# A 128-byte tile moved from the first working pool to the last one: a Fourier and Hyena encoder layer on one core

## The chip, the core and the metric

The kernel runs on one core of a Trainium2 chip. The metric is the device time of one execution in microseconds (us). Three runs of the kernel before took 2387.26, 2387.34 and 2389.71 us; their median is 2387.34 us.

## What is computed

The reference is one encoder layer, applied to two inputs of 1024 rows and 1024 channels, all in float32. Cut to what matters:

```python
p = rmsnorm(x, g_pre) @ w_in                       # 1024 x 8192: fv, fg, hv (3 parts), hg, mg (2 parts)
fz = fftn(fv in 4 groups of 256, over rows and group).real
y_f = (fz * silu(fg)) @ w_fourier_out
v, x1, x2 = split(short_conv(hv, w_short), 3)      # width 3 along the rows
z = x1 * long_conv(v, filter 0);  z = x2 * long_conv(z, filter 1)
y_h = (z * silu(hg)) @ w_hyena_out
g_f, g_h = split(sigmoid(mg + b_merge), 2)
out = x + rmsnorm((g_f * y_f + g_h * y_h) @ w_out, g_post)
```

The two long convolutions have filters as long as the sequence in both directions; the kernel makes them with small Fourier transforms written as matrix products.

## The kernel before

Every large product is made in three matmuls: a number is split into a high and a low part, and high times high, high times low and low times high are summed in PSUM (`mm3`, and `times` in the tail; both end in `mm`, line 193, so line 193 is the line of nearly all matmuls in the profile). ScalarE rounds the high part (line 170), and VectorE or GpSimd subtracts to get the low part (line 180).

There are three stages. `phase_fourier` makes the Fourier branch's transform. `phase_main` makes the filters and, in `branches`, the Hyena branch of both inputs. It also makes most input projections: `inproj` takes a stationary operand of 128 x 128 out of the tiles `wh` and `wl` (high and low part of a piece of `w_in`) and a moving operand of 128 x 512 out of the tiles `x`, which hold the whole normalised input, high and low, for all of the stage. One call has 48 such matmuls; they write the PSUM tile `pin`. `phase_tail` makes the rest with a scheme of seven block products instead of eight: the PSUM tile is `pg` for the last projections of the second input and for the output product, and `pn` for the two branches' output products. In the tail the stationary operands lie either in the old tiles `wh`, `wl` and `w`, or in others (`s1h`, `s1l`, ... `s4l`, `a2h`, `a2l`, `wa`; for `pn` in halves of the old `x` tiles and in two tiles `st0`, `st1`; the profile calls these `wh` and `wl` too, since the tile's own name is that). The moving operands are the tiles called `x`, `oB`, `n` and `room`.

What matters for the change is where these tiles lie in a partition of SBUF. The kernel opens memory pools, and the program puts each pool behind the one opened before it; inside a pool the tiles follow each other in the order in which they are first asked for. The order and the sizes per partition are:

- `cp`, constants, to byte 17,760;
- `wp`, opened by `open_x`: `wh` (3 buffers of 2048 bytes), `wl` (3 of 2048), `w` (2 of 2048), `gt` (3 of 2048), `mark` (1 of 128);
- `xp`, opened by `open_x` too: sixteen tiles of 4096 bytes, `x00` to `x17`, each with a high half and a low half of 2048 bytes;
- in `phase_main`: `mf`, `wa`, `wb`, `mi`. `mi` is the last, with `cinv` (18,432 bytes) and `cin0` (2048);
- in `phase_tail`, at the same place behind `xp`: `gs` (four `room` tiles of 16,384 bytes), `gw`, `gr`, `gt`, `op`.

A stationary operand takes 512 bytes of a partition and starts at a multiple of 512 bytes from its pool's first tile; a moving one of 512 columns takes 2048 bytes. `wp` without `mark` has 22,528 bytes, eleven times 2048. With the 128 bytes of `mark`, `xp` and all pools behind it start at 128 bytes past a multiple of 2048 from `wp`. So the distance from the stationary operand to the moving one, taken modulo 512, is:

- operands out of `wh`, `wl`, `w` of `wp` (`pin`, and two of the seven block products of `pg`): 384, that is 128 bytes short of a multiple of 512;
- all other matmuls of 512 columns (`pn`, and the other five block products of `pg`): 0, since both operands lie behind `mark`.

`mark` itself is a trick of order. The list `self.due` holds copies between tensors in DRAM that GpSimd has to issue one at a time. In `branches`, after each of the first 30 steps, GpSimd copies one column of the step's result into `mark` (line 1101) and only then issues the next copy of the list. Nobody reads `mark`.

Of the kernel before, what the change touches and what calls it, by code (L numbers as in the profile page):

```python
# [10 lines left out]
F32R = mybir.dt.float32r  # L11
# [5 lines left out]
P = 128  # L17
# [143 lines left out]
class K:  # L161
# [824 lines left out]
    def phase_main(self, nct=8, nb=NB, nf=16):  # L986
        tc, nc, a = self.tc, self.nc, self.a
        with ExitStack() as es:
            pool = lambda n: es.enter_context(tc.tile_pool(name=n, bufs=1, reuse_waits="tile"))
            self.open_mm(es, "psm")  # L990
            mf, wa, wb, mi = pool("mf"), pool("wa"), pool("wb"), pool("mi")
            ws = Rooms(wa, wb)
            with tc.issue_after(self.fz_stored.ins):
                self.load_x(0, range(4))
            self.hid = ws.tile([P, L], F32R, tag="q", name="hid", bufs=2)
            hid = ws.tile([P, L], F32, tag="q", name="hidr", bufs=2)
            for i in range(2):
                nc.sync.dma_start(hid[64 * i:64 * i + 64].rearrange("p (n t) -> p n t", n=2),
                                  self.d_h.rearrange("(n p) t -> p n t", n=2))
            with tc.issue_after(self.third[0].ins), tc.issue_after(self.third[1].ins):  # L1000
                nc.scalar.copy(self.hid, hid)
                self.sub("dve", self.hid[64:128], hid[64:128], self.hid[64:128])
            taps = self.filter_taps(0, 0, self.filter_rates(0, 0, ws), ws)
            self.load_x(0, range(4, 8))
            self.cfw0 = mf.tile([P, 4 * P], F32, name="cfw0")
            self.cfwd = mf.tile([P, 2, 12 * P], F32R, name="cfwd")
            nc.sync.dma_start(self.cfw0, a["c_fw0"])
            nc.gpsimd.tensor_copy(self.cfwd[:, 0, 0:1], self.X[4][0][1][:, 0:1])
            nc.gpsimd.dma_start(self.cfwd, a["c_fwd"])
            plain = [(5, c) for c in range(8)] + [(6, c) for c in range(8)] + [(4, c) for c in range(NH)]  # L1010
            fill = sorted([((2 * c + 1) / len(plain), t) for c, t in enumerate(plain)]
                          + [((2 * c + 1) / max(NF, 1), (0, c)) for c in range(NF)])
            fill = [t for _, t in fill]
            rates = self.filter_rates(1, 0, ws)
            self.due = self.weight_sums()
            room = mi.tile([P, 2, INVW], F32, tag="cinv", name="sums", bufs=1).rearrange("p a b -> p (a b)")
            for i in range(nf):
                if i in (3, 5, 7, 9):
                    k = (i - 3) // 2
                    r = room[:, 2048 * (k % 2):2048 * (k % 2) + 2048].rearrange("p (q n) -> p q n", q=4)  # L1020
                    self.block_sums([r[:, q] for q in range(4)], 0, k, [self.d_x[1][k + 4 * j] for j in range(2)])
                nxt = self.filter_taps((i + 1) % 2, (i + 1) // 2, rates, ws) if i + 1 < nf else None
                self.filter_spectrum(i % 2, i // 2, taps, ws)
                if i + 2 < nf:
                    rates = self.filter_rates(i % 2, i // 2 + 1, ws, self.rounded)
                taps = nxt
                for sec, c in fill[i * len(fill) // nf:(i + 1) * len(fill) // nf]:
                    self.spill_gate(0, sec, c, ws)
                if i == 12:
                    self.cinv = mi.tile([P, 2, INVW], F32R, tag="cinv", name="cinv", bufs=1)  # L1030
                    self.cin0 = mi.tile([P, 4 * P], F32, name="cin0")
                    nc.sync.dma_start(self.cin0, a["c_in0"])
                if 12 <= i < 15:

                    s = slice((i - 12) * INVW // 3, (i - 11) * INVW // 3)
                    nc.gpsimd.dma_start(self.cinv[:, :, s], a["c_inv"][:, :, s])
            self.branches(nb, nct, ws)

    def branches(self, nb, nct, ws):

        tc, nc = self.tc, self.nc
        steps = []
        for b in range(nb):
            steps.append((b, 0, 0))
            for c in range(1, nct):
                steps += [(b, 0, c), (b, 1, c - 1)]
            steps.append((b, 1, nct - 1))
        plain = list(self.PLAIN)  # L1050
        Z, X, G = {}, {}, {}

        def front(i):
            b, n, c = steps[i]
            src = self.conv(1, c, ws, "v", b) if n == 0 else Z.pop(c)
            return self.conv_front(src, ws)

        def gates(i):
            b, n, c = steps[i]
            x = self.conv(2 + n, c, ws, f"x{n + 1}", b)  # L1060
            if n and b == 0:
                early = c < NH
                ps = None if early else self.inproj(4, c)
                sg = [self.wp.tile([P, 512], F32, tag="gt", name="sg", bufs=3) for q in range(2)]
                for q in range(2):
                    s = slice(512 * q, 512 * q + 512)
                    if early:
                        nc.sync.dma_start(sg[q], self.d_g[0][4][c][:, s])
                    else:
                        nc.scalar.activation(sg[q], ps[:, s], AF.Silu)  # L1070
                G[i] = sg, early
            X[i] = x

        def close(i):

            if i in G:
                sg, early = G.pop(i)
                for q in range(2):
                    s = slice(512 * q, 512 * q + 512)
                    if early:  # L1080
                        with tc.issue_after(self.rounded.ins):
                            nc.scalar.activation(sg[q], sg[q], AF.Silu)
                    self.mul("dve", X[i][:, s], X[i][:, s], sg[q])
        B = front(0)
        gates(0)
        for i, (b, n, c) in enumerate(steps):
            nxt = None
            if i + 1 < len(steps):
                nxt = front(i + 1)
                gates(i + 1)  # L1090
                if i + 2 < len(steps) and steps[i + 2][0] != steps[i + 1][0]:
                    self.load_x(steps[i + 2][0])
            y = self.conv_back(n, c, B, ws)
            close(i + 1)
            B = nxt
            for _ in range({4: 1, 3: 1, 2: 2, 1: 2}.get(len(steps) - i, 0)):
                self.spill_gate(b, *plain.pop(), ws)
            z = self.gate(n, c, y, X.pop(i))
            if self.due:
                mark = self.wp.tile([P, 32], F32R, tag="mark", name="mark", bufs=1)  # L1100
                with tc.issue_after(nc.gpsimd.tensor_copy(mark[:, 0:1], z[:, 0:1]).ins):  # L1101
                    self.due.pop(0)()
            if n == 0:
                Z[c] = z
                continue
            nc.sync.dma_start(self.d_sh[b][c], z)
            if b == 0 and NF <= c:
                self.spill_gate(0, 0, c, ws)
        with tc.issue_after(self.ended.ins):
            for sec, c in plain:  # L1110
                self.spill_gate(1, sec, c, ws)
# [605 lines left out]
```

## Time and profile before

| | before |
|---|---|
| median of three runs | 2387.34 us |
| the profiled execution's own time | 2390.22 us |
| its span, first to last instruction | 2388.4 us |
| mean granted TensorE clock | 0.997 |
| TensorE matmul busy | 2339.0 us (98%) |
| VectorE busy | 1967.7 us (82%) |
| ScalarE busy | 1118.6 us (47%) |
| GpSimd busy | 446.4 us (19%) |
| matmuls of 128 x 512 into `pin` | 4224 |
| into `pn` | 1344 |
| into `pg` | 1680 |

A row of a group reads: line, engine, operation, tile written <- tiles read (for a matmul first the moving, then the stationary operand), shape, count; then the busy time of the group in us (overlaps counted once), the mean length of one in ns, and the idle time of the engine ahead of them. Matmuls overlap: one of 512 columns is shown some 390 ns long, and the next starts some 230 ns after it. The pitch from start to start is therefore read from the chain of waits, where a stretch of matmuls of one kind has its length and its count.

### The profile page before, as it was taken

How to read it: one execution, taken by the hardware profiler on the slowest of the kernel's cores; microseconds unless marked ns; L12 is line 12 of the kernel's file. 1: busy time of each engine (PE TensorE's matmuls, PEld its weight loads, DVE VectorE, ACT ScalarE, POOL GpSimd, SP SyncE). 2: the span in 40 equal slices, each digit the busy share in tenths (PEclk: the TensorE clock that was granted, in tenths of full speed). 3: DMA queues.
4: the chain of work that ended last, by engine and by line, in shares of the span. 5: the costliest groups of instructions: out<-in, count | busy, mean ns of one | idle time of the engine just before them, and what ended most of it. 6: DMA issues, size and time to landing. Idle time of an engine off the chain costs nothing.

```text
span 2388.4 us, 36206 instructions
## 1 busy us (share of the span) xinstructions
PE 2339.0 (98%) x12784; PEld 2019.5 (85%) x12784; DVE 1967.7 (82%) x3438; ACT 1118.6 (47%) x2080; POOL 446.4 (19%) x428
## 2 busy tenths in 40 slices
PE   6999999999999999999999999999999999999998
PEld 5989788888878888888888888888888888888787
DVE  7775687888788999999898999997765578787987
ACT  6645576676753333334222222333443464656443
POOL 3342222122223333332000000122000000101311
PEclk9999999999999999999999999999999999999999
DMA  7636765554566567667465565444954678998654
GB/s 254 208 139 218 260 212 174 177 172 151 175 218 204 186 211 211 209 194 246 161 194 150 171 193 158 151 159 159 347 165 137 221 257 267 273 313 246 198 159 141
DMA packets 246207, 479.69 MB, mean 201 GB/s; under 512 B 24582, under 2 KB 82280, under 8 KB 245706
## 3 DMA queue, kind: packets, MB, share of 16 engines
q1 hardware_dynamic: 222013, 402.25, 51.7%
q0 software_dynamic: 23792, 75.11, 11.1%
q8 instruction: 100, 1.64, 0.3%
q14 instruction: 81, 0.66, 0.1%
q10 hardware_dynamic: 221, 0.04, 0.0%
HBM read 326.82 MB, written 177.73 MB: 211 GB/s over the span
## 4 chain that ended last, share of the span: by engine, by line
PE 55%; DVE 4%; DMA 1%; issue 1%; ACT 0%; POOL 0%; DVEq 0%; SPq 0%; POOLq 0%; ACTq 0%
PE pin L193 19%; PE pg L193 14%; PE pn L193 12%; PE pT L193 5%; PE pX L193 5%; PE tph L904 1%; DMA xr<-in_x 1%; DVE x L176 0%; DMA d_m<-gt 0%; DMA k<-d_k 0%; DVE t L180 0%; DVE b L180 0%; DVE y L180 0%; DVE wl L180 0%; DVE o L176 0%
## 5 line engine op out<-in xcount | busy, mean ns | idle before, releaser
L193 PE MATMUL pin<-x,wh 128*128 128x512 f32 x2816 | 900.3, 395 | 0.0
L193 PEld LDWEIGHTS pin<-x,wh 128*128 128x128 f32 x2816 | 525.2, 189 | 107.8
L193 PE MATMUL pin<-x,wl 128*128 128x512 f32 x1408 | 556.8, 396 | 0.0
L180 POOL TENSOR_TENSOR wl<-wr,wh 128x512 fp32r<-128x512 f32 x128 | 223.5, 1747 | 696.1 <-ACT wh L170 661.3
L193 PEld LDWEIGHTS pin<-x,wl 128*128 128x128 f32 x1408 | 265.4, 189 | 52.7
L193 PE MATMUL pn<-room,wh 128*128 128x512 f32 x864 | 266.2, 389 | 0.0
L193 PEld LDWEIGHTS pn<-room,wh 128*128 128x128 f32 x864 | 162.1, 188 | 33.9 <-DVE gt L180 0.2
L193 PE MATMUL pn<-room,wl 128*128 128x512 f32 x432 | 168.4, 390 | 0.1
L180 DVE TENSOR_TENSOR t<-pX,k 128x1024 f32<-128x1024 f32 x128 | 155.6, 1215 | 11.0 <-PE pX L193 7.1
L193 PE MATMUL pX<-bh,cfwd 128*128 128x256 f32 x768 | 162.3, 288 | 0.0
L193 PE MATMUL pT<-cinv,yh 128*128 128x256 f32 x768 | 145.4, 284 | 1.9 <-DVE T0s L180 1.9
L170 ACT CAST wh<-wr 128x512 fp32r<-128x512 f32 x128 | 79.2, 618 | 135.8 <-PE pin L193 106.6
L170 ACT CAST bh<-b 128x512 fp32r<-128x512 f32 x144 | 88.3, 620 | 114.1 <-DVE b L180 83.7
L193 PEld LDWEIGHTS pT<-cinv,yh 128*128 128x128 f32 x768 | 122.7, 190 | 9.1 <-ACT T1s L957 2.0
L193 PEld LDWEIGHTS pX<-bh,cfwd 128*128 128x128 f32 x768 | 127.0, 190 | 2.7 <-issue 0.2
L1358 POOL DMA_DIRECT2D d_m<-gt x32 | 27.1, 848 | 531.9 <-DVE gt L180 502.7
L170 ACT CAST yh<-y 128x512 fp32r<-128x512 f32 x96 | 59.6, 621 | 132.2 <-DVE y L180 132.2
L193 PE MATMUL pX<-bl,cfwd 128*128 128x256 f32 x384 | 109.0, 284 | 0.0
L193 PE MATMUL pT<-cinv,yl 128*128 128x256 f32 x384 | 108.9, 284 | 0.0
L180 DVE TENSOR_TENSOR bl<-b,bh 128x512 fp32r<-128x512 f32 x144 | 103.7, 724 | 4.0 <-ACT bh L170 3.8
L1101 POOL CAST mark<-x 128x1 fp32r<-128x1 f32 x30 | 21.1, 704 | 415.6 <-DVE x L176 415.5
L180 DVE TENSOR_TENSOR y<-t 128x512 f32<-128x512 f32 x128 | 90.9, 710 | 6.8 <-PE pT L193 6.4
(362 smaller groups left out, 5174.6 us busy)
## 6 DMA issues: line engine op xcount, KB each, us to landing
k<-d_k SPq DMA_DIRECT2D x128, 512.0 KB, 4.3
wr<-in_w_in SPq DMA_DIRECT2D x128, 256.0 KB, 3.5
d_g<-gt SPq DMA_DIRECT2D x124, 256.0 KB, 2.9
wl<-d_s SPq DMA_DIRECT2D x56, 512.0 KB, 5.7
d_k<-kt SPq DMA_DIRECT2D x128, 128.0 KB, 2.2
d_k<-kt SPq DMA_DIRECT2D x64, 256.0 KB, 2.7
g<-d_g SPq DMA_DIRECT2D x64, 256.0 KB, 5.5
r<-d_g SPq DMA_DIRECT2D x60, 256.0 KB, 5.9
```

Of the source, the lines that this page charges most:

```text
L170: self.rounded = nc.scalar.copy(h, src)
L180: return e.tensor_tensor(out, a, b, op=op)
L193: return self.nc.tensor.matmul(out, lhsT, rhs, start=start, stop=stop, skip_group_check=shared)
L904: nc.tensor.transpose(tp[:, q * P:(q + 1) * P], eo[:, e, q], self.ident)
L1101: with tc.issue_after(nc.gpsimd.tensor_copy(mark[:, 0:1], z[:, 0:1]).ins):
L1358: nc.gpsimd.dma_start(dst, t, accum_op=ADD)
```

## The change

The tile `mark` goes from `wp` to `mi` and from 32 columns to the one that is used. `mi` is handed to `branches` for that.

```diff
-            self.branches(nb, nct, ws)
-
-    def branches(self, nb, nct, ws):
+            self.branches(nb, nct, ws, mi)
+
+    def branches(self, nb, nct, ws, mi):
...
             if self.due:
-                mark = self.wp.tile([P, 32], F32R, tag="mark", name="mark", bufs=1)
-                with tc.issue_after(nc.gpsimd.tensor_copy(mark[:, 0:1], z[:, 0:1]).ins):
+                mark = mi.tile([P, 1], F32R, tag="mark", name="mark", bufs=1)
+                with tc.issue_after(nc.gpsimd.tensor_copy(mark, z[:, 0:1]).ins):
                     self.due.pop(0)()
```

The program has the same instructions in the same order on each engine, with the same waits: the copy was of one column before too. What differs is addresses. `wp` stays where it was (the first `wh` buffer at byte 17,760), and everything behind it lies 128 bytes lower: the first `x` tile at byte 40,288 instead of 40,416, `room0` and `cfw0` at 105,824 instead of 105,952. `mark` now lies behind `cin0`, at byte 229,216, where nothing comes after it in `phase_main`. All matmuls of 512 columns of the last two stages have their two operands at a multiple of 512 bytes from each other then, and the starts of the tiles `wh`, `wl` and `x` are multiples of 2048 bytes apart. Distances among the tiles behind `wp` are as before.

## The prediction

> **What bounds the kernel now.** I start with the busy times of the page, then with the chain that ended last, to see which engine sets the end.
>
> ```profile
> PE 2339.0 (98%) x12784; PEld 2019.5 (85%) x12784; DVE 1967.7 (82%) x3438; ACT 1118.6 (47%) x2080; POOL 446.4 (19%) x428
> PE 55%; DVE 4%; DMA 1%; issue 1%; ACT 0%; POOL 0%; DVEq 0%; SPq 0%; POOLq 0%; ACTq 0%
> ```
>
> TensorE is busy for 98% of the span, and of the time that the chain puts on an engine nearly all is TensorE's. A busy share can hide waits, so the second view is what TensorE waited for between 200 us and the end; it has six lines in all, and these are the longest:
>
> ```profile
> PE pXf L193 <- DVE b L180: 5.5, 1, 5.5
> PE pn L765 <- DVE acc L180: 2.2, 1, 2.2
> PE pg L193 <- ACT u L1242: 1.9, 2, 1.4
> PE pT L193 <- DVE T0s L180: 1.9, 1, 1.9
> ```
>
> That is 12 us in 2200. So whatever makes matmuls shorter in that stretch shortens the kernel, unless another engine is just behind. The third view is the groups of TensorE by shape, and in it the change's subject can be seen before anything is changed:
>
> ```profile
> L193 PE MATMUL pin<-x,wh 128*128 128x512 f32 x2816 | 900.3, 395 | 0.0
> L193 PE MATMUL pin<-x,wl 128*128 128x512 f32 x1408 | 556.8, 396 | 0.0
> L193 PE MATMUL pn<-room,wh 128*128 128x512 f32 x864 | 266.2, 389 | 0.0
> L193 PE MATMUL pn<-room,wl 128*128 128x512 f32 x432 | 168.4, 390 | 0.1
> ```
>
> All four are matmuls of one shape at one granted clock. Those into `pin` take their weights from `wp` and last 395 and 396 ns; those into `pn` take them from behind `mark` and last 389 and 390 ns. The stages differ too, so this alone proves nothing. In `pg` both kinds stand in one stage, in turn:
>
> ```profile
> L193 PE MATMUL pg<-x,wh 128*128 128x512 f32 x176 | 55.3, 395 | 0.0
> L193 PE MATMUL pg<-oB,wh 128*128 128x512 f32 x120 | 37.7, 395 | 0.0
> L193 PE MATMUL pg<-x,wl 128*128 128x512 f32 x88 | 34.8, 395 | 0.0
> L193 PE MATMUL pg<-oB,wl 128*128 128x512 f32 x60 | 23.8, 397 | 0.6 <-DVE wl L180 0.6
> L193 PE MATMUL pg<-oB,w 128*128 128x512 f32 x12 | 3.0, 394 | 0.0
> L193 PE MATMUL pg<-x,s4h 128*128 128x512 f32 x96 | 29.6, 390 | 0.0
> L193 PE MATMUL pg<-oB,s4h 128*128 128x512 f32 x64 | 19.7, 390 | 0.0
> L193 PE MATMUL pg<-room,s2h 128*128 128x512 f32 x160 | 49.3, 389 | 0.0
> L193 PE MATMUL pg<-x,wa 128*128 128x512 f32 x24 | 5.6, 391 | 0.0
> ```
>
> The data `x` and `oB` occur with both kinds of weights. With `wh`, `wl` and `w` (distance 384 modulo 512) they last 394 to 397 ns, with `s4h` and `wa` (distance 0) 390 to 391 ns. So the place of the weights goes with the length, and the data, the stage and the kind of work do not. The view of the tile `pg` gives least, median and most of one matmul and of its weight load:
>
> ```profile
> L193 PEld LDWEIGHTS pg<-x,wh x176: 187/188/192, 1700.5 to 1897.7; 128*128 128x128 f32 x176
> L193 PE MATMUL pg<-x,wh x176: 390/394/404, 1700.8 to 1898.0; 128*128 128x512 f32 x176
> L193 PEld LDWEIGHTS pg<-room,s3h x160: 187/188/188, 1695.1 to 2371.0; 128*128 128x128 f32 x160
> L193 PE MATMUL pg<-room,s3h x160: 389/389/389, 1695.3 to 2371.2; 128*128 128x512 f32 x160
> ```
>
> Two things are to be seen. The weight loads have the same median, 188 ns, so loading from `wp` is not slower by itself. And the matmuls at distance 0 are all 389 ns, while those at distance 384 run from 390 to 404. An unsteady length in the matmul, with a steady load, looks like two reads that meet: the stream of moving data and the load of the next weights, which run at the same time. What decides then is how the two addresses stand to each other, and that is what the change sets.
>
> **What a matmul of 512 columns costs in time.** The lengths overlap, so the pitch decides. Three stretches of the chain, with start, length, and count:
>
> ```profile
> 1659.61 27.66 PE pin L193 x119
> 1687.28 224.92 PE pg L193 x984
> 1934.47 271.69 PE pn L193 x1198
> ```
>
> For `pin` 27.66 / 119 is 232.4 ns; for `pn` 271.69 / 1198 is 226.8 ns; `pg`, which has both kinds, lies between with 228.6 ns. The difference of the pure ones is 5.6 ns, about the 6 ns by which the lengths differ.
>
> **The sum.** First term: 4224 matmuls into `pin` (2816 + 1408) at 5.6 ns are 23.7 us. Second term: in `pg` the rows with `wh`, `wl` and `w` count 176 + 120 + 88 + 60 + 12 = 456, at 5.6 ns 2.6 us. Together 26.3 us; with 6 ns in place of 5.6 they are 28.1 us, which is the upper end.
>
> Third term, a loss: in `phase_main` the scheduler puts matmuls into `pin` in short stretches between narrower ones, and no row shows how a 512-column matmul at distance 0 fares beside those. The nearest row is `pg<-oB,s4h`, 390 ns on the average where the undisturbed ones have 389: it follows the products out of `wp`, and the difference is what a change of stream leaves behind. Bounds are nothing, and 1 ns on each of the 4224 matmuls, which is 4.2 us; I take 1.7 us, nearer to nothing, since much of that 1 ns comes from the old distance and goes with it.
>
> Fourth term: VectorE. Where TensorE becomes shorter, VectorE has to keep up. The windows of 100 us show where that is tight (window, then TensorE, its loads, VectorE, ScalarE, GpSimd):
>
> ```profile
> 700.00:800.00 100.00, 100.00 (x579) 87.56 (x578) 86.08 (x139) 37.10 (x69) 29.78 (x35) 1.00 0.62 198
> 800.00:900.00 100.00, 100.00 (x591) 88.09 (x590) 99.91 (x153) 36.03 (x67) 41.59 (x44) 1.00 0.64 201
> 900.00:1000.00 100.00, 98.13 (x591) 86.36 (x590) 96.87 (x152) 33.66 (x61) 27.91 (x36) 1.00 0.71 215
> 1000.00:1100.00 100.00, 100.00 (x586) 87.75 (x586) 100.00 (x162) 36.37 (x68) 35.48 (x36) 1.00 0.65 191
> 1100.00:1200.00 100.00, 100.00 (x569) 87.05 (x568) 90.47 (x150) 34.40 (x62) 5.80 (x7) 1.00 0.61 208
> 1500.00:1600.00 100.00, 100.00 (x599) 88.39 (x598) 97.95 (x167) 33.66 (x64) 19.79 (x15) 1.00 0.52 164
> ```
>
> And the same windows with the matmuls into `pin` alone, for their counts:
>
> ```profile
> 800.00:900.00 100.00, 65.94 (x271) 49.42 (x270) 15.22 (x12) 6.54 (x6) 1.00 0.64 201
> 900.00:1000.00 100.00, 62.22 (x249) 44.92 (x248) 12.73 (x11) 5.57 (x5) 1.00 0.71 215
> 1000.00:1100.00 100.00, 68.52 (x275) 49.69 (x274) 12.69 (x10) 6.65 (x7) 1.00 0.65 191
> ```
>
> From 800 to 1100 us VectorE idles for only 0.1 + 3.1 + 0 = 3.2 us. There TensorE is to save 795 x 5.6 ns = 4.5 us. At worst all of it is lost, at best nothing: VectorE may lag some microseconds and catch up after 1100 us, where it idles 10 us in 100. I take a loss of 1.5 us. After 2300 us the chain ends in VectorE and a DMA, but only the few `pg` matmuls out of `wp` lie there; I take nothing.
>
> Everything else costs nothing. The mark itself stays the same instruction:
>
> ```profile
> L1101 POOL CAST mark<-x 128x1 fp32r<-128x1 f32 x30 | 21.1, 704 | 415.6 <-DVE x L176 415.5
> ```
>
> It writes one column now as before, 30 times 0.7 us, on an engine that waits for VectorE most of the time; no wait, issue or DMA moves.
>
> The sum is 26.3 - 1.7 - 1.5 = 23.1 us, about 1%. The profiled execution's 2390.22 us would become 2367; the median of the runs, 2.9 us lower, 2387.34 - 23.1 = **2364 us**.
>
> **The rivals.**
>
> *The distance is not the cause, or the loads do not meet the stream.* Then the 6 ns belong to something else that goes with `wp`, such as tiles that ScalarE and GpSimd are writing while their neighbours are read, and the time stays at 2387 us. Against it: the matmuls out of `wp` are 394 to 397 ns in every row, whatever the engines around them do, and `pn` reads its weights out of freshly written tiles at 389. [...] Chance 9%.
>
> *VectorE becomes the bound.* If VectorE's work sets the pace wherever it is over 90% now, the gain from 700 to 1600 us is mostly lost: about 2400 matmuls (270 a window by the rows above) at 5.6 ns are 13.4 us, of which the sum has given up 1.5. What remains is some 11 us, 2376 us. For it speak the two windows with no idle time; against it that TensorE had one wait of 1.9 us for VectorE in all of that stretch. It decides if VectorE runs without a lead. Chance 12%.
>
> *The place itself is slow, not the distance (slower than before).* All fast matmuls now have weights 128 bytes past `wp`'s grid of 512 bytes, all slow ones lie on the grid. If a start on that grid is the slow one, the change puts the weights of `pn` (1344) and the other 1224 of `pg` on it: 2568 x 5.6 ns = 14.4 us more, with `pin` as slow as before, 2402 us. The condition is that the grid of 512 bytes is counted from zero and not from the other operand. Against it: the weight loads take 188 ns in either place. The trace has no fast matmul with both operands on that grid, so it isn't excluded. Chance 7%.
>
> **How the numbers follow.** The forecast has 72%, VectorE 12%, no effect 9%, the slow place 7%. About 0.2% (5 us) is what a measurement of this kernel can tell from no change. Faster by more than that are the first two, 84%; the same 9%; slower 7%. The range begins at 2357 us (28.1 us gained, no loss, and 2 us for narrower matmuls beside `pin`, whose own pitch may gain) and ends at 2381, with VectorE's case and some room for a part of the effect; outside lie the last two rivals, 16%.
>
> **What would show it.** In the profile after, the rows `pin<-x,wh` and `pg<-x,wh` should read 389 to 391 ns, with least and most close together, and a long stretch of `pin` in the chain should have a pitch of 227 to 228 ns; `pn` and `s4h` should stay at 389 and 390. If `pin` falls and the time does not, the waits of TensorE for VectorE between 800 and 1600 us will have grown, and that step was wrong. If `pn` rises to 395, the place was the cause. If `pin` stays at 395, the distance was not.

## The result and the profile after

| | before | after |
|---|---|---|
| median of six runs each | 2387.30 us (2384.61 to 2389.71) | 2371.95 us (2370.30 to 2373.83) |
| the profiled execution's own time | 2390.22 us | 2372.98 us |
| its span | 2388.4 us | 2371.2 us |
| mean granted TensorE clock | 0.997 | 0.996 |

The ratio is 0.9937, with a 95% interval of 0.9924 to 0.9950: 15.4 us or 0.63% faster. The forecast was 2364 us, a gain of 23.1 us; the range of 2357 to 2381 holds the time, and the gain is a third smaller than forecast.

The busy times of the page after, and the chain by engine:

```profile
PE 2321.9 (98%) x12784; PEld 2016.9 (85%) x12784; DVE 1970.2 (83%) x3438; ACT 1118.7 (47%) x2080; POOL 446.3 (19%) x428
PE 54%; DVE 4%; issue 2%; DMA 1%; POOL 0%; ACT 0%; DVEq 0%; SPq 0%; POOLq 0%; ACTq 0%
```

TensorE does the same 12,784 matmuls with 17.1 us less busy time (2339.0 before) and is still the bound. VectorE, ScalarE and GpSimd have the counts and, within 3 us, the busy times of before. So the gain is in the matmuls. (PEld is the loading of weights; in a long stretch after the change the matmuls of 512 columns start 227 ns apart at a granted clock of 1.00, and 430 ns apart at 0.50.) The groups by shape show which (columns: the group, then its busy time and the mean length of one in ns):

```profile
L193 PE MATMUL pin<-x,wh 128*128 128x512 f32 x2816 | 889.7, 391 | 0.0
L193 PE MATMUL pin<-x,wl 128*128 128x512 f32 x1408 | 552.0, 392 | 0.0
L193 PE MATMUL pn<-room,wh 128*128 128x512 f32 x864 | 266.4, 389 | 0.6 <-DVE gt L180 0.6
L193 PE MATMUL pg<-x,wh 128*128 128x512 f32 x176 | 54.2, 389 | 0.0
L193 PE MATMUL pg<-oB,wl 128*128 128x512 f32 x60 | 23.5, 391 | 0.3 <-DVE wl L180 0.3
L193 PE MATMUL pg<-x,s4h 128*128 128x512 f32 x96 | 29.6, 389 | 0.0
```

The products out of `wp` in `pg` fell from 394 to 397 ns to 389 to 391, all of the difference. Those at distance 0 before stayed, `pn` at 389 and `s4h` at 390 before and 389 now. But `pin`, nine tenths of the matmuls that the change is about, fell only from 395 and 396 to 391 and 392, not to 389. The view of the tile `pg` (least, median, most) has lost its spread:

```profile
L193 PEld LDWEIGHTS pg<-x,wh x176: 187/188/188, 1684.2 to 1879.6; 128*128 128x128 f32 x176
L193 PE MATMUL pg<-x,wh x176: 389/389/389, 1684.4 to 1879.8; 128*128 128x512 f32 x176
```

390/394/404 has become 389/389/389, with the weight loads as before. Where `pin` lost its part is seen when stretches of the chain are laid beside each other (start, length, count). The order of instructions is the same, so each stretch of before has its twin. First before, then after:

```profile
1235.20 2.77 PE pin L193 x12
1064.00 4.64 PE pin L193 x20
1093.07 5.58 PE pin L193 x24
1242.98 14.40 PE pin L193 x62
```

```profile
1223.27 2.75 PE pin L193 x12
1053.84 4.56 PE pin L193 x20
1082.74 5.47 PE pin L193 x24
1231.02 14.08 PE pin L193 x62
...
1643.99 27.00 PE pin L193 x119
```

The longest stretch gained 27.66 - 27.00 = 0.66 us, and 119 x 5.6 ns is 0.67: there the first term holds in full. At 62 matmuls the gain is 0.32 us of 0.35, at 24 it is 0.11 of 0.13, at 20 it is 0.08 of 0.11, and at 12 it is 0.02 of 0.07. So what is missing is not a part of each matmul but some 25 to 45 ns for each stretch. In the long stretch it is hidden by the price: from its thirteenth matmul on, a stretch has 232.6 ns from start to start before and 226.7 after, which is 5.9 and not 5.6. The groups in two windows of after say the same, first 700 to 1600 us, where `pin` comes in short stretches, then 1640 to 1670, where it comes in one:

```profile
L193 PE MATMUL pin<-x,wh 128*128 128x512 f32 x1605 | 510.4, 392 | 0.0
```

```profile
L193 PE MATMUL pin<-x,wh 128*128 128x512 f32 x80 | 24.8, 389 | 0.0
```

The second loss is waiting. TensorE's two largest waits after, from 200 us to the end (us in total, times, longest):

```profile
PE pXf L193 <- DVE b L180: 5.9, 2, 5.5
PE pT L193 <- DVE T0s L180: 3.6, 2, 2.2
```

The wait of `pT` for VectorE has grown most, from 1.9 us to 3.6. Two waits of `pn` for VectorE at the tail, 1.1 and 0.6 us, are new, and all of TensorE's waits from 200 us on add up to 15.8 us, where they were 12.5. The timeline of TensorE at the longest piece of `pT`'s wait (start, length, instruction, idle time before it) shows that the wait has a sequel:

```profile
975.40 0.76 PE L193 MATMUL pT<-cinv,yh 128*128 128x256 f32 x2 [2.19 <-DVE T0s L180]
...
976.39 0.63 PE L193 MATMUL pin<-x,wh 128*128 128x512 f32 x1
976.82 0.63 PE L193 MATMUL pin<-x,wl 128*128 128x512 f32 x1
...
979.57 0.39 PE L193 MATMUL pin<-x,wl 128*128 128x512 f32 x1
```

After 2.19 us of waiting, the matmuls are 0.63 us long and start 0.43 us apart, nearly twice their usual spacing, until about 978.8 us: 3.4 us at half pace, 1.7 us lost. The window that holds it has a granted clock of 0.98 (the column after GpSimd's), where it was 1.00 before:

```profile
900.00:1000.00 100.00, 96.35 (x552) 83.50 (x553) 98.77 (x155) 33.66 (x60) 31.52 (x40) 0.98 0.65 201
```

In it TensorE begins 552 matmuls (591 before). Half pace is not new, though. Before, TensorE ran at half pace for 6.8 us from 691 us on, behind its wait of 5.5 us; after, it did so for 3.4 us from 682 us on, behind the same wait. Between 200 and 2300 us the two executions thus have the same 6.8 us of it, and what the change lost there is the 3.3 us of waits.

### The profile page after: what moved, and what is told of

Its sections match the earlier page's. It is cut to its first block, busy times and chain, and to the rows that moved or that the text cites. A ratio compares the mean times of both kernels' runs of the same rounds, so it can differ in the third digit from the quotient of the medians.

```text
span 2371.2 us, 36206 instructions
## 1 busy us (share of the span) xinstructions
PE 2321.9 (98%) x12784; PEld 2016.9 (85%) x12784; DVE 1970.2 (83%) x3438; ACT 1118.7 (47%) x2080; POOL 446.3 (19%) x428
## 4 chain that ended last, share of the span: by engine, by line
PE 54%; DVE 4%; issue 2%; DMA 1%; POOL 0%; ACT 0%; DVEq 0%; SPq 0%; POOLq 0%; ACTq 0%
PE pin L193 18%; PE pg L193 14%; PE pn L193 10%; PE pT L193 5%; PE pX L193 5%; PE tph L904 1%; DVE x L176 0%; DMA k<-d_k 0%; DMA d_m<-gt 0%; DVE t L180 0%; POOL d_m L1358 0%; DVE b L180 0%; DMA wl<-d_s 0%; DVE y L180 0%; DMA xr<-in_x 0%
## 5 line engine op out<-in xcount | busy, mean ns | idle before, releaser
L193 PE MATMUL pin<-x,wh 128*128 128x512 f32 x2816 | 889.7, 391 | 0.0
```

Source lines behind the costliest of these rows:

```text
L193: return self.nc.tensor.matmul(out, lhsT, rhs, start=start, stop=stop, skip_group_check=shared)
```

## The experiments

The theory to be tested: the distance from weights to data decides, because the stream of data and the next weight load meet; what is missing is a settling after each change of stream, and a lead of VectorE that is used up. Rivals: something else that goes with `wp`, such as neighbours being written; the place and not the distance; and VectorE as the main loss.

**Matmuls alone, by distance.** The kernel is 48 matmuls for each distance between weights and data in one big tile, first with 512 columns (`wide`), with both operands moved by the same amount (`both`), then with 256 columns (`half`), and at the end stretches of 24 wide ones after 12 narrow ones, at distance 0 (`same`) and 384 (`off`). The number in a name counts how far the weights lie past the data, modulo 512. The kernel's old 384 is meant in the same way: its weights are 128 bytes short of the data, and counted from weights to data it would be 128. At 128 and 384 this makes no difference (232.5 ns at both), at 64 and 448 it does (233.3 and 229.0). The core of it:

```python
w = 128 * k + (1024 if r == 2 else 0) + s + o          # s = distance / 4, o = common shift / 4
x = 4096 + 1024 * (k % 7) + 512 * (r == 1) + o
nc.tensor.matmul(p[:, 0:n], big[:, w:w + P], big[:, x:x + n], start=j == 0, stop=j == count - 1)
```

> This kernel leaves out the whole layer: it copies both inputs to the outputs and runs groups of matmuls alone, with nothing else at work, to price the distance by itself. Groups wideN: 48 matmuls of 512 columns whose weights lie N bytes past a multiple of 512 bytes from the data (modulo 512; 512, 640, 896 and 1024 ask whether the period is 512). halfN: the same with 256 columns. bothN: distance 0, with weights and data together N bytes further on. Then 12 matmuls of 256 columns ahead of 24 of 512, at distance 0 (same) and at 384 (off). If the distance decides: wide0, wide512, wide1024 and all bothN have a pitch of 227 ns, wide384 and wide896 some 232 to 233 with lengths of 390 to 404 ns, and wide128 and wide640 are equal to each other. If something else that goes with the pool decides (neighbouring writes by other engines): all groups have 227 ns, since nothing is written here. If settling after narrow matmuls is what was lost in the changed kernel: the first five matmuls of each group same take 233, 236, 228, 232 and 231 ns and the rest 227, 25 ns in all. Open, with no expectation from the rows: whether some distance is better than 0 at 256 or 512 columns.

The chain of that kernel (start, length, name with the distance in bytes, count):

```profile
51.70 7.26 PE wide0w L29 x32
...
70.15 11.20 PE wide64w L29 x48
...
92.59 11.16 PE wide128w L29 x48
103.75 10.99 PE wide192w L29 x48
114.74 10.90 PE wide256w L29 x48
125.64 11.20 PE wide320w L29 x48
136.84 11.16 PE wide384w L29 x48
...
203.14 10.89 PE both128b L29 x48
...
235.86 5.75 PE half0h L29 x48
...
264.27 5.65 PE half192h L29 x48
...
317.15 5.47 PE same L29 x24
...
344.75 5.58 PE off L29 x24
```

At distances 0 and 256 a matmul costs 7.26 / 32 = 226.9 and 10.90 / 48 = 227.1 ns. At 128 and 384 it costs 232.5, at 64 and 320 it costs 233.3, at 192 it costs 229.0. Moved together by 128 bytes (226.9), the operands are as fast as at distance 0. So it is the distance, in periods of 256 bytes, and not the place; no other engine works beside them, so no neighbour needs to write. 5.6 ns for the kernel's old distance of 384 is what the prediction used. The place of the weights alone changes the matmuls' pace by 6 ns in 227.

The last two rows answer for the settling. 24 wide matmuls after narrow ones take 5.47 us at distance 0, and at the settled 226.7 ns they would take 5.44: 0.03 us for one change. At 384 they take 5.58, as 24 x 232.4 ns would. So the fast distance pays for a change of stream and the slow one doesn't: 24 matmuls gain 0.11 us and not 0.13, which is the kernel's own pair of rows with x24. Narrow matmuls go the other way: 119.8 ns at distance 0 and 117.7 at 192.

**The distance without the move.** The kernel before, with the old tile of 32 columns asked for first in `wp` (the added line stands in `open_x`, behind the line that opens the pool) and not last. Every tile behind `wp` lies where it lay before, `wh`, `wl` and `w` lie 128 bytes higher, and the distance is a multiple of 512.

```diff
+        self.mark = self.wp.tile([P, 32], F32R, tag="mark", name="mark", bufs=1)
...
-                mark = self.wp.tile([P, 32], F32R, tag="mark", name="mark", bufs=1)
-                with tc.issue_after(nc.gpsimd.tensor_copy(mark[:, 0:1], z[:, 0:1]).ins):
+                with tc.issue_after(nc.gpsimd.tensor_copy(self.mark[:, 0:1], z[:, 0:1]).ins):
```

> The old mark of 32 columns, in wp as before, but as the first tile of wp and not the last: wh and wl lie 128 bytes higher, everything behind wp at the places of the kernel before, and the distance of wh and wl to the data is 0 modulo 512. The instructions and their order are those of the kernel before. If the distance is what counts: the rows of pin fall from 395 and 396 to 391 and 392 ns as in the changed kernel, pg<-x,wh to 389, and the time is 2372 us (15 gained). If it was something else in the change (the one-column tile, its place in the last pool, or the places of all the tiles behind wp): pin stays at 395 and the time at 2387.

Median of five 2370.78 us against 2388.05 for the kernel before on that chip; ratio 0.9929 (0.9916 to 0.9941). The group and the long stretch:

```profile
L193 PE MATMUL pin<-x,wh 128*128 128x512 f32 x2816 | 891.1, 392 | 0.0
```

```profile
1644.27 27.00 PE pin L193 x119
```

The whole gain is there with `mark` in the old pool and at the old size. What the change does to `mi`, to the size of the tile and to the places behind `wp` is worth nothing that these times could show.

**Half the tile.** `mark` in `wp` with 16 columns, so that everything behind `wp` lies 64 bytes past the grid and the weights lie 64 bytes short of a multiple of 512 from the data, 448 in the count of the matmuls alone.

```diff
-                mark = mi.tile([P, 1], F32R, tag="mark", name="mark", bufs=1)
-                with tc.issue_after(nc.gpsimd.tensor_copy(mark, z[:, 0:1]).ins):
+                mark = self.wp.tile([P, 16], F32R, tag="mark", name="mark", bufs=1)
+                with tc.issue_after(nc.gpsimd.tensor_copy(mark[:, 0:1], z[:, 0:1]).ins):
```

> The kernel before with a mark of 16 columns in place of 32, so 64 bytes: the weights lie 64 bytes short of a multiple of 512 from the data (448 modulo 512). The matmuls measured alone have 228.8 ns there against 232.4 at 384 and 226.7 at 0. If that table holds in the kernel: 4680 matmuls gain up to 3.6 ns, 16.8 us, less what VectorE and the settling take, as in the changed kernel: 2374 us, within 3, and pg<-x,wh at some 391 ns. If only multiples of 512 are good: 2387 us and 394 to 395 ns.

Median of five 2375.16 us, ratio 0.9944 (0.9931 to 0.9957); the median lies between those of the two kernels.

```profile
L193 PE MATMUL pin<-x,wh 128*128 128x512 f32 x2816 | 893.5, 393 | 0.0
```

```profile
1644.16 27.24 PE pin L193 x119
```

27.24 / 119 is 228.9 ns; the matmuls alone had 10.99 / 48 = 229.0 at 448. The pace at a distance carries over from matmuls alone to the kernel. `pg<-x,wh` fell to 393 ns only, not to the 391 expected; the matmuls alone have 392 there.

**VectorE relieved.** In both kernels 16 products on VectorE (`X` times `sg`, in the Hyena branch) are left out, so that VectorE can't hold TensorE up between 700 and 1700 us. The program orders itself anew around them, so the two are compared with each other.

```diff
-                    self.mul("dve", X[i][:, s], X[i][:, s], sg[q])
```

> The kernel before without the 16 products of VectorE in close (the second gate of the first input's Hyena branch is left out, so 16 x 0.72 = 11.5 us less for VectorE between 680 and 1100 us). The scheduler makes another order of it, the same in the two kernels of this pair, so the pair is read as a difference. If VectorE takes back part of the change: this kernel alone gains little, 2 to 3 us (its one long wait of 1.9 us), 2384.

> The changed kernel without the same 16 products of VectorE. If VectorE's lack of idle time between 800 and 1100 us is what took 3 to 4 us of the 19.4 that the pitch of the matmuls gives: the difference between this one and its partner of before is 18 to 20 us, 2365. If the loss lies elsewhere (the tail, the clock by chance, the run to run spread of the first 200 us): the difference is 15 us again, 2369.

Medians 2384.45 us (11 runs) and 2364.03 us (4 runs), ratios 0.9987 (0.9978 to 0.9996) and 0.9899 (0.9884 to 0.9914) to the same kernel before; between them lie 20.4 us. Neither has a wait of TensorE for VectorE between 700 and 1700 us, and the window of the half pace is full, with 590 matmuls before and 602 after. The row of after with less work:

```profile
900.00:1000.00 100.00, 100.00 (x602) 89.14 (x601) 99.21 (x160) 37.52 (x69) 44.76 (x42) 1.00 0.65 207
```

So VectorE took some of the gain: up to 5 us by the first set's medians (20.4 less 15.4), and less in later sets. With it out of the way the gain is 20.4 us, still short of 26.3.

**The changed kernel again.** Run beside the kernel with narrow matmuls off distance 0 (below), without an edit, to see how steady the loss to VectorE is.

> The changed kernel once more, on the same chip and against the same runs of the kernel before as the two gaps: 2371 us, pin at 391 and 392 ns. Whether TensorE's half clock of 3.4 us behind the wait at some 973 us comes again: if VectorE causes the wait, the wait of 2 us comes again, with or without the clock.

Median of five 2368.73 us (2368.40 to 2370.60) against 2387.58 before, ratio 0.9922 (0.9909 to 0.9934): 18.9 us. In its profile the wait for `T0s` is 1.60 us, no half pace follows, and the window from 900 to 1000 us has 578 matmuls and a clock of 1.00:

```profile
900.00:1000.00 100.00, 98.39 (x578) 86.85 (x577) 98.57 (x153) 33.68 (x60) 34.98 (x42) 1.00 0.66 202
```

The stretches have the lengths of the first profile, to 0.01 us (x12 2.75, x20 4.56, x54 12.27, x119 27.00). All waits of TensorE from 200 us on add up to 11.8 us here, less than the 12.5 of the kernel before. So the gain in pace is fixed and the loss to VectorE varies from execution to execution, down to nothing.

**Changes of stream alone.** Two kernels of matmuls alone, in cycles of 12 wide, 6 narrow, 12 wide, 6 narrow. The first moves the narrow ones' distances (and at the end the wide ones' to 128 and 384), the second tries eleven combinations of places for the narrow ones, to see which of them spare the wide ones the settling. Cores of the two edits to the kernel of matmuls alone:

```diff
+        for s in (0, 32, 64, 96, 128, 160, 192, 224):
+                group(f"wide{s}x", 512, 12, 0, 0)
+                group(f"fore{s}x", 256, 6, 0, s)
+                group(f"wide{s}t", 512, 12, 0, 0)
+                group(f"back{s}t", 256, 6, s, 2 * s)
```

```diff
+CASES = (("A", 0, 0, 0, 0), ("B", 0, 64, 64, 128), ("C", 0, 192, 192, 384), ("D", 128, 64, 64, 0), ("E", 64, 0, 128, 64),
+          ("F", 64, 0, 64, 0), ("G", 128, 64, 128, 64), ("H", 96, 0, 96, 0), ("I", 96, 32, 96, 32), ("J", 64, 0, 0, 0), ("K", 0, 0, 64, 0))
...
+                group(f"fore{t}x", 256, 6, mf, wb)
+                group(f"back{t}t", 256, 6, wa, mi)
```

> The layer is left out again: matmuls alone, now in the mixture of phase_main. Cycles of 12 matmuls of 512 columns (weights and data at distance 0), 6 of 256 like those into pX (their data N bytes higher than their weights), 12 of 512, 6 of 256 like those into pT (weights N, data 2N bytes higher); N is 0, 32, 64, 96, 128, 160, 192 or 224. At the end the same with the weights of the 512-column ones at 128 and at 384 and the narrow ones at 0. From the first bench: narrow matmuls take 120.0 ns at distance 0 and 117.7 at 64 and 192, so a cycle with N = 64 should be 12 x 2.3 = 28 ns shorter than with N = 0 if the settling of the wide ones after them stays at 25 ns, and up to 50 ns shorter or longer if the settling changes with N. With 384 for the wide ones a cycle should be longer than with 0 by 24 x 5.7 less two settlings of 25 ns, 87 ns.

> The layer is left out once more; the cycles of the second bench (12 wide, 6 as into pX, 12 wide, 6 as into pT) with other places of the four pools, in bytes modulo 256 for mf (weights of pX), wb (data of pX), wa (weights of pT), mi (data of pT). A all 0 and B (0, 64, 64, 128) and C (0, 192, 192, 128) repeat the second bench: 6920, 6893 and 6853 ns a cycle. In C the weights lie 64 bytes past the data, narrow matmuls take 117.7 ns and the wide ones behind them 227 from the first. If it is the sign of the distance in the narrow ones that spares the settling, all cases with 64 past (D, E, F, G) have some 6853 ns, whatever the pools' places are to the wide operands; if it is the distance between the last narrow data and the first wide weights, only some of them have it. H and I ask for 96 past, J and K for one of the two kinds alone, which should lie half way, 6885.

Rows of the first, for narrow matmuls at distance 0 and at 192, and for wide ones at 128:

```profile
76.52 2.75 PE wide0t L25 x12
...
325.90 2.72 PE wide192t L25 x12
...
405.34 2.77 PE wide128f L25 x12
```

These are the kernel's own figures for a stretch of 12: 2.75 us after the change and 2.77 before. Start to start, the five wide matmuls after a change are 233, 236, 228, 233 and 230 ns apart in the rows `same` of the first kernel of matmuls alone (233, 236, 228, 232 and 231 in the changed kernel), and 227 from then on. At 128 there is no settling: the first are 230 ns apart, and it stays near 232. So a stretch of 12 gains 0.02 us and not 0.07. A whole cycle gained 53 ns (6973 to 6920) where I had expected 87, because I had priced 24 matmuls at the full difference, and 12 at 128 take 2.77 us and not 12 x 232.4 ns = 2.79. With the data of the narrow ones 64 to 96 bytes past their weights the cycle is shorter (6893 and 6894 ns), as expected, and at 192 (6853) the settling is gone as well. At 64 half of it is gone: wide stretches behind the second kind of narrow ones take 2.72 us, those behind the first kind 2.76. My guess on what spares it, the sign of the narrow distance, fell in the second kernel: of the combinations D to G, for which it should have been spared, none had it (6906 and 6907 ns, with 6894 for B). Only C had, which is the 192 of the first kernel again. Weights 96 bytes past the data gave 6907 (H) and 7000 ns (I), and one kind alone 6914 (J and K), where half way, 6885, was expected.

**Narrow matmuls off distance 0.** The changed kernel with gaps of 64 bytes, so that the data of `pX` and `pT` lie 64 bytes past their weights and not at distance 0 (192 in the count of the matmuls alone), while `pin` keeps its own: an unused tile at the start of `mi`, and `mark`, now 64 bytes, at the end of `mf`.

```diff
+            mi.tile([P, 16], F32, tag="pad", name="pad", bufs=1)
...
-            self.branches(nb, nct, ws, mi)
+            self.branches(nb, nct, ws, mf)
...
-                mark = mi.tile([P, 1], F32R, tag="mark", name="mark", bufs=1)
-                with tc.issue_after(nc.gpsimd.tensor_copy(mark, z[:, 0:1]).ins):
+                mark = mi.tile([P, 16], F32R, tag="mark", name="mark", bufs=1)
+                with tc.issue_after(nc.gpsimd.tensor_copy(mark[:, 0:1], z[:, 0:1]).ins):
```

> The changed kernel with two gaps of 64 bytes more: the mark as a tile of 64 bytes at the end of mf, and an unused tile of 64 bytes at the start of mi. Then weights and data of the narrow matmuls (pX, pXf, pT; 2880 in all) lie 64 bytes short of a multiple of 256 from each other, where matmuls measured alone take 117.7 ns and not 120.0; the 512-column ones stay at distance 0. Same instructions, same order. If the distance rules these too and TensorE still sets the end: 2880 x 2.3 ns = 6.6 us less than the changed kernel, less what VectorE takes back between 800 and 1100 us: 2367 us. If the settling gets longer by as much, or VectorE takes it all: 2371 us.

Median of five 2365.95 us, ratio 0.9911 (0.9898 to 0.9925), 2.8 us less than the changed kernel beside it (2368.73). The groups of the changed kernel in that set, then of this one:

```profile
L193 PE MATMUL pX<-bh,cfwd 128*128 128x256 f32 x768 | 162.2, 288 | 0.0
L193 PE MATMUL pT<-cinv,yh 128*128 128x256 f32 x768 | 145.5, 284 | 1.6 <-DVE T0s L180 1.6
```

```profile
L193 PE MATMUL pX<-bh,cfwd 128*128 128x256 f32 x768 | 160.3, 285 | 0.0
L193 PE MATMUL pT<-cinv,yh 128*128 128x256 f32 x768 | 143.8, 282 | 1.6 <-DVE T0s L180 1.6
```

3 and 2 ns less each, as matmuls alone have it (119.8 to 117.7 at 192). The intervals overlap, so the gain over the changed kernel rests on the rows more than on the times. It is the fastest complete kernel of the study.

**Gaps of 192 bytes.** For the combination without settling the constants need another order, so the tile `db` goes into the buffer of `w3` first, in a partner without the gaps; the gaps of 192 bytes come on top. In the diff the first pair of lines is the partner's, the rest is the edit with the gaps.

```diff
-        db = ws.tile([P, P], F32, tag="db", name="db", bufs=1)
+        db = ws.tile([P, 256], F32, tag="w3", name="db", bufs=1)[:, 0:P]
...
+            mi.tile([P, 48], F32, tag="pad", name="pad", bufs=1)
...
-            self.branches(nb, nct, ws, mi)
+            self.branches(nb, nct, ws, mf)
...
-                mark = mi.tile([P, 1], F32R, tag="mark", name="mark", bufs=1)
-                with tc.issue_after(nc.gpsimd.tensor_copy(mark, z[:, 0:1]).ins):
+                mark = mi.tile([P, 48], F32R, tag="mark", name="mark", bufs=1)
+                with tc.issue_after(nc.gpsimd.tensor_copy(mark[:, 0:1], z[:, 0:1]).ins):
```

> The changed kernel with the tile db (512 bytes) in the buffer of w3, which frees 512 bytes of a partition. The scheduler makes another order of it. It is the partner of the next kernel and is expected near the changed kernel: 2370 us, within 6; all distances are those of the changed kernel, so pin at 391 and 392 ns, with the first five matmuls of 512 columns behind narrow ones at 233, 236, 228, 232 and 231 ns.

> The same with two gaps of 192 bytes, one behind mf (the mark) and one ahead of mi: the weights of the narrow matmuls lie 64 bytes past a multiple of 256 from their data, the case C of the third bench (6853 ns a cycle against 6920). TensorE's order is the partner's, word for word; VectorE's differs at the tail's beginning in a few rows. If the settling behind narrow matmuls is what the changed kernel's pin has left: pin falls to 389 to 390 ns, its first matmuls in a stretch have 227, and the narrow ones 281 to 282 ns; that is 6 us for pin and 6 for the narrow ones less than the partner, of which VectorE may take some 3 between 800 and 1100 us. If the settling was not due to the places: pin stays at 391 to 392 and 3 to 6 us are gained by the narrow ones alone.

Two misses. The partner takes 2392.25 us (11 runs, ratio 1.0021, 1.0012 to 1.0030), not about 2370: with a shared buffer the program orders itself anew, and TensorE has new waits. From 200 us on they add up to 28.4 us, against 15.8 in the changed kernel, and the granted clock is 0.994 against 0.996. The two largest:

```profile
PE pXf L193 <- DVE kt L176: 5.7, 4, 2.4
PE pin L193 <- DVE v L176: 4.9, 1, 4.9
```

With the gaps it takes 2386.78 us (11 runs, ratio 1.0002, 0.9993 to 1.0010), 5.5 us less than the partner. How much of that is the gaps' is open, since VectorE's order differs between the two as well. `pX` went from 288 to 286 ns and `pT` from 284 to 283, and `pin` stayed at 393:

```profile
L193 PE MATMUL pin<-x,wh 128*128 128x512 f32 x2816 | 892.8, 393 | 3.5 <-DVE v L176 3.5
```

389 or 390 would have shown the settling gone. This mean holds stretches of half pace too, so the starts outside them say more: from start to start a `pin` matmul takes 228.4 ns in the partner and 228.1 here. Over the first five matmuls of a stretch behind `pX`, the settling fell from 26 ns to 14; behind `pT` it stayed. So the places that spare it for matmuls alone take off only a part of it here. In the kernel `pin` also follows products other than `pX` and `pT` (in the changed kernel 191 of 300 changes to `pin` come from these two, by my count in the trace, the others from `pft`, `tph`, `pXf` and a few more); whether those bring the settling back wasn't tried.

## Why the prediction was right, and where its size was wrong

- **The mechanism: right, and shown.** The distance decides: `pg<-x,wh` went from 390/394/404 to 389/389/389, matmuls alone have the same 5.6 ns with no other engine of the core at work, moving the weights and not the data gives the same gain, and a distance between gives the time between. The trace of before also shows which load counts. In `pg`, a matmul whose own weights lie at distance 0 and whose successor's lie in `wp` starts 232.6 ns ahead of that successor (18 of them), where one between neighbours at distance 0 takes 226.9: it is slowed while the next weights are loaded. That two reads meet was my guess and fits this; the runs show that the distance decides and the period of 256 bytes, not what lies behind it.
- **The second term, 2.6 us in `pg`: right.** 456 matmuls at 394 to 397 ns went to 389 to 391, some 6 ns or 2.7 us.
- **The first term, 23.7 us in `pin`: right per settled matmul** (119 of them gained 0.66 us where 5.6 ns each make 0.67), and not reached on the whole.
- **The third term, 1.7 us for the change of stream: this step failed.** I took the bounds from `pg<-oB,s4h`, a row from a stage with no narrow matmuls, as a surcharge of up to 1 ns on each matmul. That 1 ns came from the old distance alone: the row has 389 ns after the change. The cost in `phase_main` is per change: 300 changes at about 25 ns would be 7.5 us, and stretches of fewer than five pay less. By the groups, `pin` gained 4 ns x 4224 = 16.9 us, so the term was 23.7 - 16.9 = 6.8 us, above its upper bound of 4.2. The trace of before couldn't show the settling, since the old distance has none, but the share of short stretches could have been counted.
- **The fourth term, 1.5 us for VectorE: of the right kind, and unsteady.** In the profiled execution TensorE's waits from 200 us on grew by 3.3 us, 1.7 of them at `T0s`, in the stretch named, and 1.7 in the new waits of `pn` at the tail, where I had taken nothing. In the repeat they didn't grow. The half pace wasn't in the sum at all; between these two executions it about cancels.
- **The sum as measured:** 16.9 + 2.7 - 3.3 = 16.3 us, against 17.2 between the two profiled executions, 15.4 between the medians of that set, and 17.3 and 18.9 in later sets for the same distance. With VectorE out of the way the gain was 20.4 us, near the first two terms as measured, 16.9 + 2.7 = 19.6 us.
- **The rivals.** No effect of the distance, at 2387 us, falls with the first experiment. The slow place, at 2402, falls too: after the change weights of all kinds lie on the grid, and `pn` stays at 389 ns. VectorE as the bound, at 2376, was a part of the truth: the wait was the one named, the price was at most 5 us and not the 13.4 that the rival put on it.

## What to carry to other kernels

When the weights of one matmul are loaded while the data of another are read, look at the distance between the two addresses: here multiples of 256 bytes were 2.5% faster for 512 columns than 128 bytes off them (226.9 against 232.5 ns), and a small tile of 128 bytes in a pool ahead of the data had set it for 4680 matmuls. Groups of one shape with two lengths, one steady and one with a spread (389 ns, and 390 to 404), are how it showed in the profile. And a gain per instruction, measured in a long stretch, should be multiplied only by the instructions that stand in long stretches; those behind a change of shape need a price of their own, per change (some 25 ns here).

## What the runs showed of the hardware that was not expected

- **Settling.** At the fast distance the first five matmuls of 512 columns after narrower ones start 233, 236, 228, 232 and 231 ns apart and only then 227; at distance 128 or 384 there is nothing to settle (in the kernel before the first five are 230 to 232 ns apart). For matmuls alone one combination of places (case C, with the narrow matmuls' data 192 bytes past their weights) spares it whole, at 6853 ns a cycle against 6920, and others in part (6893); in the kernel that one took off a part, 12 of 26 ns behind `pX`. What decides is open.
- **The best distance depends on the shape.** Wide matmuls are fastest at 0 modulo 256 bytes (226.7 ns settled, 233.3 at 64), narrow ones slowest there (119.8 against 117.7 at 192).
- **Half pace after a short wait.** The length of a wait alone didn't decide here. In the kernel with half the tile a wait of 1.07 us is followed by half pace, in the one with narrow matmuls off distance 0 a wait of 2.61 us isn't. Windows of 3.41 us, first of the former, then of the latter (TensorE's busy time stands first, the granted clock behind GpSimd's):

```profile
2193.99:2197.40 3.41, 1.88 (x8) 0.97 (x7) 3.38 (x6) 1.85 (x3) 0.84 (x1) 1.00 1.03 417
2197.40:2200.81 3.41, 3.41 (x10) 2.68 (x9) 3.34 (x6) 0.26 (x1) 0.85 (x1) 0.50 1.04 382
...
266.79:270.20 3.41, 1.90 (x9) 1.25 (x7) 3.41 (x6) 1.59 (x4) 1.82 (x1) 1.00 1.00 315
270.20:273.61 3.41, 2.31 (x14) 2.12 (x15) 1.61 (x6) 2.03 (x5) 0.00 (x0) 1.00 1.03 369
```

In the clock records of the traces of the two kernels, the stretches of half pace begin whole multiples of 3.413 us apart within an execution: at 46.00, 691.12 and 2384.13 us before (189 and 496 of them), at 33.29, 681.82, 975.37 and 2368.00 us after (190, 86 and 408). Cut into windows at these multiples, from 100 us on and up to 20 us before the end, the two executions have three windows at full clock with over 1.8 us of TensorE's idle time, wait by wait added up (3.38 us before, 3.41 and 2.15 after). Each was followed by half pace, and none of the windows with less was, up to one of 1.78 us before. Yet in the kernel with half the tile a window with 3.41 - 1.88 = 1.53 us was, by the rows above, so the idle time in one window doesn't settle it alone; what does is open. The wait of 2.61 us lies in two windows, with 1.51 and 1.10 us, and both have a clock of 1.00. The same wait in the kernel before lies in two as well, with 1.20 and 1.04 us, and the third has a clock of 1.00 like them.
